# Strassen MLP on one core: four products held in PSUM banks over all chunks of a layer, banks given out by kind

## The chip, the cores and the metric

One Trainium2 chip; the program runs on one NeuronCore of it. The metric is device time in microseconds (us), the median of several executions. One further execution was recorded by the profiler; its own time stands beside its span below. Engines: TensorE (PE in the rows; PEld is its weight load), VectorE (DVE), ScalarE (ACT), GpSimd (POOL), SyncE (SP).

## The reference, cut to what matters

A decoder trunk of two layers on 256 tokens of width 2048, in float32. Each layer has a mixer (convolution and sparse attention in layer 0, causal pooling in layer 1) and then an MLP:

```python
def mlp(x, g, w1, w2):
    h = rmsnorm(x, g) @ w1          # 2048 -> 8192
    h = jnp.square(jax.nn.relu(h))
    return h @ w2                   # 8192 -> 2048
...
        x = x + mlp(x, mlp_norm[layer], w_mlp_in[layer], w_mlp_out[layer])
    return rmsnorm(x, final_norm)
```

## The kernel before

**Numbers in two parts.** Every weight tile W (128 x 2048, 1 MB) is streamed from HBM into `wraw` and split: ScalarE writes the rounded part `whi` (L147), VectorE the rest, `wlo = W - whi` (L152), in two halves of 1024 columns each. A product then needs three matmuls for each pair of blocks: x-high by W-high, x-high by W-low, x-low by W-high. There are three buffers each of `wraw`, `whi` and `wlo`.

**The MLP in chunks.** The hidden width of 8192 is cut into 8 chunks of 1024. For a chunk, the hidden tiles (`tile_of`: 48 matmuls of 256 columns into a bank, called *g* below) are computed one chunk ahead; `hidden` (L1023) takes the bank's relu and square into SBUF on ScalarE. The second matrix then multiplies the chunk's hidden values by seven products per half of the output (index `s`, two halves per chunk) instead of eight, in the way of Strassen and Winograd: two token blocks (of 128) by two output blocks of 512 columns. A *product* is 12 matmuls of 512 columns into one PSUM bank. Its inputs are the quarters of the hidden values (`f11`, `f12`, `f22`) or sums of them (`s1` to `s4`), each split in two by ScalarE (L1070) and VectorE (L1073); sums of weights are made in place on VectorE (`z += b`, `z += wraw`, L116) and by DMAs that add (L123, L127). The last of the eight chunks is done plainly, so the Strassen loop (L1143) makes seven passes per layer, c = 0 to 6, each of two halves, with 8 g and 14 products per pass. The flag `plain` marks the pass c = 6.

**What happens to a product.** PSUM has 8 banks of 128 x 512. `bank3` (L969) hands them out in turn. After each product, `update` (L1113) adds the bank, scaled for each token by 1/rms, onto the residual `x` in SBUF: one VectorE instruction of 128 x 512. A half makes seven updates. Three products accumulate in one bank A with f11 (`s2`, `s3`, `f22` after `f11`) and are added after each step, `s4` accumulates onto `s1` in bank C; the bank is added to one block after s1 and to another after s4. B holds f12.

**Order.** Each engine runs its instructions in the order in which the code issues them. `W.next()` (L170), called at the start of each g and product, first issues the loads of the unit four ahead and then the splits of all units up to two ahead; queued steps that make the inputs (`make`, `make_sum`) are put between the halves of the splits (L150). So in VectorE's order an update stands behind the splits that its product's `W.next()` issued, and ahead of those of the next unit. The order of one half, as TensorE sees it: f11, g, f12, s1, g, s2, s4, g, s3, g, f22.

Of the kernel before, what the change touches and what calls it, by code (L numbers as in the profile page):

```python
# [27 lines left out]
F32 = mybir.dt.float32  # L28
# [4 lines left out]
PSUM = bass.MemoryType.PSUM  # L33

P = 128
S = 256
# [143 lines left out]
def trunk(ctx: ExitStack, tc: tile.TileContext, a: dict, out: bass.AP, dump: dict | None = None):  # L180
# [10 lines left out]
    def mm(out, w, x, **kw):  # L191
        n = int(np.prod(x.shape[1:]))
        pe[0] += max(4 * n / 2400, 0.214) if x.dtype == F32 else max(n / 2400 + 0.0025, 0.107)
        nc.tensor.matmul(out, w, x, **kw)  # L194
# [81 lines left out]
    with ExitStack() as mx:  # L276
        mix = mx.enter_context(tc.tile_pool(name="mix", bufs=1, side="right", reuse_waits="tile"))
        ps1 = mx.enter_context(ExitStack())
        ps = ps1.enter_context(tc.tile_pool(name="ps1", bufs=1, space=PSUM, reuse_waits="tile"))

        def acc1(n=256, dt=F32):
            return ps.tile([P, 512], dt, tag="acc", bufs=8, name="acc")[:, 0:n]
# [181 lines left out]
        for pr in range(2):  # L464
            for i in range(2):
                acc = acc1()
# [140 lines left out]
        ps = ps2.enter_context(tc.tile_pool(name="ps2", bufs=1, space=PSUM, reuse_waits="tile"))  # L607
# [259 lines left out]
        for j in range(8):  # L867
# [5 lines left out]
            acc = ab[j][:, 0:256]  # L873
# [90 lines left out]
            nc.sync.dma_start(dump["o_tok"], o_tok)  # L964
        ps2.close()

        ps = ctx.enter_context(tc.tile_pool(name="ps3", bufs=1, space=PSUM, reuse_waits="tile"))

        def bank3():  # L969
            return ps.tile([P, 512], F32, tag="acc", bufs=8, name="acc")  # L970

        x = act.tile([P, 2, D], F32, tag="xr", bufs=1, name="x")
        turns = []
# [24 lines left out]
    def ssq_tile():  # L998
        return mlp.tile([P, 2, 4], F32, tag="ssq", bufs=2, name="ssq")

    def add_squares(dc, ssq):

        for tok in range(2):
            j = mlp.tile([P, 512], mybir.dt.bfloat16, tag="sq", bufs=1, name="sq")
            nc.scalar.activation(j, x[:, tok, dc * 512:(dc + 1) * 512], AF.Square, accum_out=ssq[:, tok, dc:dc + 1])
# [14 lines left out]
    def form(tag):  # L1020
        return mlp.tile([P, 1024], F32R, tag=tag, bufs=1, name=tag)

    def hidden(acc, out):  # L1023

        nc.scalar.activation(out, acc, AF.Relu)  # L1025
        nc.scalar.activation(out, out, AF.Square)  # L1026

    def unit_wide(acc):

        hi, lo = W.next(16)  # L1030
        for k in range(16):
            Xh, Xl = (xT[k // 4][:, k % 4, i * 256:(i + 1) * 256] for i in range(2))
            mm(acc, hi[:, k], Xh, start=(k == 0), stop=False)
            mm(acc, hi[:, k], Xl, start=False, stop=False)
            mm(acc, lo[:, k], Xh, start=False, stop=(k == 15))

    def t_tile():
        return mlp.tile([P, 4, 256], F32, tag="t", bufs=3, name="t")
# [24 lines left out]
    def quarter(c, tok, half):  # L1063
        return T[c, half][:, :, tok * P:(tok + 1) * P]

    def make(tag, src):

        def rounded():
            F[tag] = form(tag).rearrange("p (k t) -> p k t", k=4)
            nc.scalar.activation(F[tag][:, :, 0:P], src(), AF.Copy)  # L1070

        def rest():
            vector.tensor_sub(F[tag][:, :, P:2 * P], src(), F[tag][:, :, 0:P].bitcast(F32))  # L1073
            pending.remove(tag)

        pending.append(tag)
        W.queue += [rounded, rest]

    def make_sum(c, tag):
        def add():  # L1080
            s = sums[tag] = mlp.tile([P, 4, P], F32, tag="s", bufs=3, name="s")
            if tag == "s1":
                vector.tensor_sub(s, quarter(c, 1, 0), quarter(c, 1, 1))
            elif tag == "s2":
                vector.tensor_sub(s, sums["s1"], quarter(c, 0, 0))
            elif tag == "s3":
                vector.tensor_sub(s, quarter(c, 0, 0), quarter(c, 1, 0))
            else:
                vector.tensor_add(s, sums["s2"], quarter(c, 0, 1))

        W.queue.append(add)
        make(tag, lambda: sums[tag])

    def made(tag):
        while tag in pending:
            W.queue.pop(0)()
        return F[tag]

    def product(acc, tag, first):
        hi, lo = W.next()  # L1100
        X = made(tag)
        for k in range(4):
            xh, xl = X[:, k, 0:P], X[:, k, P:2 * P]
            mm(acc, xh, hi[:, k], start=(first and k == 0), stop=False, skip_group_check=True)
            mm(acc, xh, lo[:, k], start=False, stop=False, skip_group_check=True)
            mm(acc, xl, hi[:, k], start=False, stop=(k == 3), skip_group_check=True)

    def run_mlp(after, first):
        ssq = ssq_tile()
        r2 = const.tile([P, 2], F32, tag="r2", bufs=2, name="r2")  # L1110
        nr2 = const.tile([P, 2], F32, tag="nr2", bufs=2, name="nr2")

        def update(tok, dc, acc, r=r2):  # L1113
            o = x[:, tok, dc * 512:(dc + 1) * 512]
            vector.scalar_tensor_tensor(o, acc, r[:, tok:tok + 1], o, op0=ALU.mult, op1=ALU.add)

        def tile_of(c, j):

            if j % 4 == 0:
                T[c, j // 4] = t_tile()  # L1120
            acc = bank3()[:, 0:256]
            unit_wide(acc)
            hidden(acc, T[c, j // 4][:, j % 4])

        for _ in first():
            pass
        make("f11", lambda: quarter(0, 0, 0))
        make_sum(0, "s3")
        for j in range(4, 8):
            tile_of(0, j)  # L1130
            add_squares(j - 4, ssq)
        vector.reciprocal(r2, token_ms(ssq))
        vector.tensor_scalar(nr2, r2, -1.0, None, op0=ALU.mult)

        def second_half(c):
            make("f12", lambda: quarter(c, 0, 1))
            if c < CHUNKS - 1:
                for tag in ("s1", "s2", "s4"):
                    make_sum(c, tag)

        second_half(0)
        make("f22", lambda: quarter(0, 1, 1))
        for c in range(CHUNKS - 1):  # L1143
            plain = c + 1 == CHUNKS - 1
            for s in range(2):
                d0, d1 = 2 * s, 2 * s + 1
                A, C = bank3(), bank3()
                n = [4 * s]

                def g():  # L1150
                    tile_of(c + 1, n[0])
                    n[0] += 1

                product(A, "f11", True)
                update(0, d0, A)
                if s:
                    make("f11", lambda c=c: quarter(c + 1, 0, 0))
                g()
                B = bank3()
                product(B, "f12", True)  # L1160
                update(0, d0, B)
                product(C, "s1", True)
                update(1, d1, C)
                if s and plain:
                    make("s1", lambda c=c: quarter(c + 1, 1, 0))
                g()
                product(A, "s2", False)
                update(0, d1, A, nr2)
                product(C, "s4", False)
                update(0, d1, C)  # L1170
                g()
                product(A, "s3", False)
                update(1, d1, A, nr2)
                if s and not plain:
                    make_sum(c + 1, "s3")
                g()
                if s:
                    second_half(c + 1)
                product(A, "f22", False)
                update(1, d0, A)  # L1180
            make("f22", lambda c=c: quarter(c + 1, 1, 1))


        later = []
        for dc in range(4):
            acc = [bank3() for _ in range(2)]
            for half in range(2):
                hi, lo = W.next()
                X = [made(tag) for tag in (("f11", "s1"), ("f12", "f22"))[half]]
                order = [(k, tok) for k in range(4) for tok in range(2)]  # L1190
                if half:
                    order.sort(key=lambda o: o[1])
                for k, tok in order:
                    xh, xl = X[tok][:, k, 0:P], X[tok][:, k, P:2 * P]
                    mm(acc[tok], xh, hi[:, k], start=(half == 0 and k == 0), stop=False)
                    mm(acc[tok], xh, lo[:, k], start=False, stop=False)
                    mm(acc[tok], xl, hi[:, k], start=False, stop=(half == 1 and k == 3))
                if half == 0:
                    while later:
                        later.pop(0)()  # L1200
            for tok in range(2):
                update(tok, dc, acc[tok])
            later += after(dc)
        return later
# [104 lines left out]
    for h in range(2):  # L1309
        c = slice(h * 1024, (h + 1) * 1024)  # L1310
# [117 lines left out]
```

## Time and profile before

| | |
|---|---|
| median of 3 runs | 1772.74 us (1771.68 to 1776.7) |
| the profiled execution | 1777.96 us, span 1776.2 us |
| TensorE's granted clock over the span | 0.997 |
| busy shares | TensorE 99%, weight loads 90%, VectorE 85%, ScalarE 61%, GpSimd 3% |
| the MLP of layer 0, of layer 1 | about 392 to 1031 us and 1106 to 1731 us of the span |

The profiled execution lies 5.22 us above the median. Busy time of TensorE is modelled for pipelined matmuls, so 99% says that matmuls overlap without holes, not that they run at peak. The rows below are read as: start in us from the span's start, duration, engine, line, operation, output and inputs by the program's names; in brackets the engine's idle time before it and what ended that.

### The profile page before, as it was taken

What the parts mean: (1) busy time and instruction counts of PE and PEld (TensorE: products, weight loads), DVE (VectorE), ACT (ScalarE), POOL (GpSimd) and SP (SyncE); (2) the same over time, 40 slices, a digit from 0 to 9 for tenths busy, and PEclk for the clock granted to TensorE, in tenths of its full rate; (3) what the DMA queues carried; (4) which work ended last, traced back from release to release, by engine and by line L of the source; (5) the groups of instructions that cost most, each with busy time, mean ns of one, the idle gap of its engine ahead of it and who ended that gap; (6) DMA issues with size and microseconds to landing.
All of it is one profiled execution on the core that took longest, in us unless ns stands there. A gap on an engine that the chain in (4) does not pass through costs nothing.

```text
span 1776.2 us, 28729 instructions
## 1 busy us (share of the span) xinstructions
PE 1752.6 (99%) x11726; PEld 1595.4 (90%) x11726; DVE 1518.5 (85%) x1888; ACT 1084.6 (61%) x1626; POOL 59.7 (3%) x80
## 2 busy tenths in 40 slices
PE   9999999999999999999999999999999999999997
PEld 7999998889898899999898989988989898989885
DVE  6998997766989898898989868798988989898984
ACT  4445666547666666666666655766666666666663
POOL 1000000000000000000000000000000000000000
PEclk9999999999999999999999999999999999999998
DMA  7654323546778787878777764687878787778772
GB/s 274 237 197 143 120 96 134 199 167 227 259 248 253 236 248 236 276 230 295 232 248 247 230 228 155 232 256 238 257 237 271 233 294 233 249 243 259 247 245 97
DMA packets 58052, 399.89 MB, mean 225 GB/s; under 512 B 6560, under 2 KB 6960, under 8 KB 10816
## 3 DMA queue, kind: packets, MB, share of 16 engines
q1 hardware_dynamic: 47760, 333.47, 48.9%
q0 software_dynamic: 8576, 61.43, 18.5%
q10 hardware_dynamic: 1584, 3.16, 0.5%
q8 instruction: 92, 1.51, 0.3%
q14 instruction: 40, 0.33, 0.0%
HBM read 395.93 MB, written 2.10 MB: 224 GB/s over the span
## 4 chain that ended last, share of the span: by engine, by line
PE 78%; DVE 18%; ACT 2%; issue 1%; DMA 1%; ACTq 0%; POOLq 0%; SPq 0%; DVEq 0%
PE acc L194 73%; DVE wlo L78 9%; DVE z L78 3%; DVE s L78 3%; PE S L194 2%; DVE x L78 2%; PE PV L194 1%; ACT whi L147 1%; PE T L232 1%; PE acc L232 1%; DVE f L78 0%; DMA xraw<-in_xT 0%; ACT t L1026 0%; DMA ident<-in_ident 0%; ACT t L1025 0%
## 5 line engine op out<-in xcount | busy, mean ns | idle before, releaser
L194 PE MATMUL acc<-xT,whi 128*128 128x256 f32 x4992 | 872.1, 279 | 0.0
L194 PEld LDWEIGHTS acc<-xT,whi 128*128 128x128 f32 x4992 | 764.8, 188 | 10.1
L78 DVE TENSOR_TENSOR wlo<-wraw,whi 128x1024 fp32r<-128x1024 f32 (+1 forms) x552 | 604.9, 1126 | 143.7 <-ACT whi L147 142.8
L194 PE MATMUL acc<-xT,wlo 128*128 128x256 f32 x2496 | 694.0, 278 | 0.0
L147 ACT ACTIVATE whi<-wraw 128x1024 fp32r<-128x1024 f32 (+1 forms) x552 | 515.2, 974 | 105.1 <-PE acc L194 86.5
L194 PEld LDWEIGHTS acc<-xT,wlo 128*128 128x128 f32 x2496 | 470.7, 189 | 0.0
L194 PE MATMUL acc<-whi,s 128*128 128x512 f32 x960 | 318.5, 393 | 2.8 <-DVE s L78 1.6
L78 DVE TENSOR_TENSOR wlo<-z,whi 128x1024 fp32r<-128x1024 f32 x224 | 267.1, 1219 | 47.9 <-ACT whi L147 47.1
L147 ACT ACTIVATE whi<-z 128x1024 fp32r<-128x1024 f32 x224 | 230.5, 1054 | 94.2 <-DVE z L78 73.3
L194 PE MATMUL acc<-whi,f 128*128 128x512 f32 x864 | 283.0, 392 | 0.0
L194 PEld LDWEIGHTS acc<-whi,s 128*128 128x128 f32 x960 | 179.3, 188 | 42.2 <-DVE s L78 7.5
L1025 ACT ACTIVATE t<-acc 128x256 f32<-128x256 f32 x128 | 48.8, 381 | 251.6 <-PE acc L194 250.8
L194 PE MATMUL acc<-wlo,s 128*128 128x512 f32 x480 | 190.8, 397 | 1.1
L194 PEld LDWEIGHTS acc<-whi,f 128*128 128x128 f32 x864 | 162.4, 188 | 32.2
L194 PE MATMUL acc<-wlo,f 128*128 128x512 f32 x432 | 169.4, 392 | 0.0
L78 DVE SCALAR_TENSOR_TENSOR x<-acc,r,x 128x512 f32<-128x512 f32 x156 | 116.4, 746 | 14.4 <-PE acc L194 14.2
L194 PEld LDWEIGHTS acc<-wlo,s 128*128 128x128 f32 x480 | 90.1, 188 | 28.2 <-DVE wlo L78 9.7
L78 DVE SCALAR_TENSOR_TENSOR ctile<-ctile,cw 128x256 f32<-128x256 f32 x240 | 101.5, 475 | 0.1
L194 PEld LDWEIGHTS acc<-wlo,f 128*128 128x128 f32 x432 | 81.1, 188 | 16.0
L1070 ACT ACTIVATE s<-s 128x512 fp32r<-128x512 f32 x56 | 35.4, 632 | 72.1 <-DVE s L78 72.1
L78 DVE TENSOR_TENSOR z<-z,wraw 128x1024 f32<-128x1024 f32 x56 | 65.9, 1219 | 0.0
L78 DVE TENSOR_TENSOR z<-z,b 128x1024 f32<-128x1024 f32 x56 | 65.9, 1219 | 0.0
(206 smaller groups left out, 1361.4 us busy)
## 6 DMA issues: line engine op xcount, KB each, us to landing
wraw<-in_ws SPq DMA_DIRECT2D x254, 1024.0 KB, 6.3
z<-in_ws SPq DMA_DIRECT2D x28, 1024.0 KB, 7.4
b<-in_ws SPq DMA_DIRECT2D x28, 1024.0 KB, 4.8
b<-in_ws POOLq DMA_DIRECT2D x28, 1024.0 KB, 8.8
z<-in_ws POOLq DMA_DIRECT2D x28, 1024.0 KB, 8.2
xraw<-in_xT SPq DMA_DIRECT2D x4, 512.0 KB, 7.5
wraw<-in_ws SPq DMA_DIRECT2D x8, 256.0 KB, 7.4
w<-in_cmp_w POOLq DMA_DIRECT2D x2, 1024.0 KB, 7.6
```

The lines of the kernel that those rows point to most:

```text
L78: return fn(*args, **kw)
L147: nc.scalar.activation(hi[:, c], raw[:, c], AF.Copy)
L194: nc.tensor.matmul(out, w, x, **kw)
L232: nc.tensor.transpose(out, src, ident[0:n, 0:n])
L1025: nc.scalar.activation(out, acc, AF.Relu)
L1070: nc.scalar.activation(F[tag][:, :, 0:P], src(), AF.Copy)
```

## The change

Bank roles become fixed for the Strassen loop: the old pool is closed (`banks_for`), and a pool `strassen` gives two banks B (one per half), two banks S (`S1`, `S4`), two banks A, one C and one G, eight in all. The f12 products of both halves, and in half 0 the products s1 and s4, stay in banks of their own (B[0], B[1], S1, S4) over all seven passes: they start a bank only at c = 0 and are added to x only at c = 6. Since s4 no longer accumulates onto s1 there, S1 is added to two blocks at c = 6 and S4 to one. Half 1 keeps C as before. All g share the one bank G, where before each took the next of eight. After the loop a third pool (`ps4`) gives banks in turn again. Layer 1 goes through the same two pool changes. The products, the splits, the sums and the loads are unchanged in number and order.

```diff
--- before.py
+++ after.py
@@ -964,10 +964,18 @@
             nc.sync.dma_start(dump["o_tok"], o_tok)
         ps2.close()
 
-        ps = ctx.enter_context(tc.tile_pool(name="ps3", bufs=1, space=PSUM, reuse_waits="tile"))
-
-        def bank3():
-            return ps.tile([P, 512], F32, tag="acc", bufs=8, name="acc")
+        ps3 = ctx.enter_context(ExitStack())
+        banks = []
+
+        def banks_for(name):
+
+            ps3.close()
+            banks[:] = [ps3.enter_context(tc.tile_pool(name=name, bufs=1, space=PSUM, reuse_waits="tile"))]
+
+        def bank3(tag="acc", bufs=8):
+            return banks[0].tile([P, 512], F32, tag=tag, bufs=bufs, name="acc")
+
+        banks_for("ps3")
 
         x = act.tile([P, 2, D], F32, tag="xr", bufs=1, name="x")
         turns = []
@@ -1114,11 +1122,11 @@
             o = x[:, tok, dc * 512:(dc + 1) * 512]
             vector.scalar_tensor_tensor(o, acc, r[:, tok:tok + 1], o, op0=ALU.mult, op1=ALU.add)
 
-        def tile_of(c, j):
+        def tile_of(c, j, *bank):
 
             if j % 4 == 0:
                 T[c, j // 4] = t_tile()
-            acc = bank3()[:, 0:256]
+            acc = bank3(*bank)[:, 0:256]
             unit_wide(acc)
             hidden(acc, T[c, j // 4][:, j % 4])
 
@@ -1140,15 +1148,20 @@
 
         second_half(0)
         make("f22", lambda: quarter(0, 1, 1))
+
+        banks_for("strassen")
+        B = [bank3("B", 2) for _ in range(2)]
+        S1, S4 = (bank3("S", 2) for _ in range(2))
         for c in range(CHUNKS - 1):
             plain = c + 1 == CHUNKS - 1
             for s in range(2):
                 d0, d1 = 2 * s, 2 * s + 1
-                A, C = bank3(), bank3()
+                A = bank3("A", 2)
+                C = bank3("C", 1) if s else S1
                 n = [4 * s]
 
                 def g():
-                    tile_of(c + 1, n[0])
+                    tile_of(c + 1, n[0], "G", 1)
                     n[0] += 1
 
                 product(A, "f11", True)
@@ -1156,18 +1169,22 @@
                 if s:
                     make("f11", lambda c=c: quarter(c + 1, 0, 0))
                 g()
-                B = bank3()
-                product(B, "f12", True)
-                update(0, d0, B)
-                product(C, "s1", True)
-                update(1, d1, C)
+                product(B[s], "f12", c == 0)
+                if plain:
+                    update(0, d0, B[s])
+                product(C, "s1", s or c == 0)
+                if s or plain:
+                    update(1, d1, C)
                 if s and plain:
                     make("s1", lambda c=c: quarter(c + 1, 1, 0))
                 g()
                 product(A, "s2", False)
                 update(0, d1, A, nr2)
-                product(C, "s4", False)
-                update(0, d1, C)
+                product(C if s else S4, "s4", not s and c == 0)
+                if s or plain:
+                    update(0, d1, C)
+                if plain and not s:
+                    update(0, d1, S4)
                 g()
                 product(A, "s3", False)
                 update(1, d1, A, nr2)
@@ -1179,6 +1196,8 @@
                 product(A, "f22", False)
                 update(1, d0, A)
             make("f22", lambda c=c: quarter(c + 1, 1, 1))
+
+        banks_for("ps4")
 
 
         later = []
```

## Rows read from the trace of the kernel before

**Rows 1.** The page, parts 1 and 4: busy time and the chain by line.

```profile
PE 1752.6 (99%) x11726; PEld 1595.4 (90%) x11726; DVE 1518.5 (85%) x1888; ACT 1084.6 (61%) x1626; POOL 59.7 (3%) x80
...
PE acc L194 73%; DVE wlo L78 9%; DVE z L78 3%; DVE s L78 3%; PE S L194 2%; DVE x L78 2%; PE PV L194 1%; ACT whi L147 1%; PE T L232 1%; PE acc L232 1%; DVE f L78 0%; DMA xraw<-in_xT 0%; ACT t L1026 0%; DMA ident<-in_ident 0%; ACT t L1025 0%
```

**Rows 2.** The chain that ended last, in time: start, us, what.

```profile
534.05 58.60 PE acc L194 x394
...
787.45 57.36 PE acc L194 x394
...
1242.86 57.37 PE acc L194 x394
...
1326.09 57.37 PE acc L194 x394
```

**Rows 3.** Waits of TensorE's weight loads, 425 to 1730 us: total, times, longest.

```profile
PEld acc L194 <- DVE wlo L78: 9.7, 21, 0.6
PEld acc L194 <- DVE s L78: 7.5, 14, 1.2
```

**Rows 4.** Windows: stretch, length; busy PE, PEld, DVE, ACT, POOL; clock, DMA share, GB/s.

```profile
892.25:933.34 41.09, 41.09 (x278) 37.66 (x276) 36.21 (x38) 26.47 (x33) 1.70 (x2) 1.00 0.79 256
640.53:682.45 41.92, 41.92 (x277) 38.40 (x276) 36.30 (x38) 26.45 (x33) 1.71 (x2) 1.00 0.80 252
903.21:914.17 10.96, 10.96 (x74) 9.98 (x73) 10.53 (x12) 8.73 (x10) 0.85 (x1) 1.00 0.98 298
441.17:453.23 12.06, 11.25 (x73) 9.90 (x72) 12.06 (x14) 9.71 (x13) 0.85 (x1) 1.00 0.84 243
```

**Rows 5.** Timeline of the weight loads, pass c = 6 of layer 0.

```profile
951.49 0.19 PEld L194 LDWEIGHTS acc<-wlo,s 128*128 128x128 f32 x1 [0.39 <-DVE wlo L78]
...
953.28 0.19 PEld L194 LDWEIGHTS acc<-wlo,s 128*128 128x128 f32 x1 [0.57 <-DVE wlo L78]
953.89 0.30 PEld L194 LDWEIGHTS acc<-whi,s 128*128 128x128 f32 x2 [0.42 <-DVE s L78]
```

**Rows 6.** Timeline of VectorE before those waits.

```profile
929.86 2.36 DVE L78 TENSOR_TENSOR wlo<-wraw,whi 128x1024 fp32r<-128x1024 f32 x2 [1.72 <-ACT whi L147]
...
947.22 0.74 DVE L78 SCALAR_TENSOR_TENSOR x<-acc,r,x 128x512 f32<-128x512 f32 x1
947.88 0.68 DVE L78 TENSOR_TENSOR s<-s,s 128x512 fp32r<-128x512 f32 x1
...
951.36 0.74 DVE L78 SCALAR_TENSOR_TENSOR x<-acc,r,x 128x512 f32<-128x512 f32 x1
952.02 1.21 DVE L78 TENSOR_TENSOR wlo<-wraw,whi 128x1024 fp32r<-128x1024 f32 x1
```

**Rows 7.** Groups by line and form, VectorE: the updates.

```profile
L78 DVE SCALAR_TENSOR_TENSOR x<-acc,r,x 128x512 f32<-128x512 f32 x156 | 116.4, 746 | 14.4 <-PE acc L194 14.2
...
L78 DVE SCALAR_TENSOR_TENSOR x<-acc,nr,x 128x512 f32<-128x512 f32 x56 | 41.8, 746 | 0.0
```

**Rows 8.** Timeline of ScalarE, two relus of g and what follows.

```profile
951.82 0.36 ACT L1025 ACTIVATE t<-acc 128x256 f32<-128x256 f32 x1
...
961.99 0.39 ACT L1025 ACTIVATE t<-acc 128x256 f32<-128x256 f32 x1 [3.14 <-PE acc L194]
...
962.73 4.02 ACT L147 ACTIVATE whi<-z 128x1024 fp32r<-128x1024 f32 x4
```

**Rows 9.** Timeline of TensorE: an earlier change of pools, and a g.

```profile
335.39 0.40 PE L194 MATMUL S<-whi,yo 128*128 128x512 f32 x1
335.63 0.39 PE L194 MATMUL acc<-whi,yc 128*128 128x512 f32 x1
...
961.67 0.28 PE L194 MATMUL acc<-xT,wlo 128*128 128x256 f32 x1
...
964.53 0.28 PE L194 MATMUL acc<-xT,whi 128*128 128x256 f32 x1
```

## Prediction

> **What bounds the kernel now.** I read four views in this order. First the page: TensorE is busy 99% of the span, VectorE 85%, and the chain of work that ended last lies 73% on matmuls into banks and about 18% on VectorE's weight splits, sums and updates [rows 1]. So TensorE is nearly the bound, and VectorE sets the pace in places. The reader should ask how much TensorE really loses there, since a busy share cannot say it.
>
> Second, the chain in time. It repeats once per pass of the Strassen loop: some 57 us of matmuls, then a run of VectorE work, then matmuls again. From one entry to the next is the length of a pass: 1326.09 - 1242.86 = 83.23 us; in a stretch of layer 0 three passes take 787.45 - 534.05 = 253.40 us, 84.47 each [rows 2].
>
> Third, windows cut where TensorE does not wait. From the start of one g to the same g half a pass later it needs 41.09 us, so a pass without waiting is 2 x 41.09 = 82.18 us, and a pass of 83.23 us holds 1.05 us of waiting. In the stretch of layer 0 the half takes 41.92 us, a pass 83.84, and the waiting is 84.47 - 83.84 = 0.63 us [rows 4]. The whole loss is small: TensorE's weight loads waited 9.7 us for weight splits and 7.5 us for the inputs `s` over both MLPs [rows 3]; not all of that is lost, because a weight load normally runs ahead of its matmul. That is the most the change can touch. Shortening VectorE's work is worth only what TensorE waits for it.
>
> Fourth, one pass in detail. The three waits of a pass stand close together, at 951.49, 953.28 and 953.89 us, in the products s2 and s4 of half 0, and all end on VectorE [rows 5]. VectorE's last idle time before them is the 1.72 us ahead of 929.86, where it waits for ScalarE; from there to the waits it is dense [rows 6], because both weight sums, four input sums and the normal splits fall together. It slowly loses its lead of two units, and TensorE catches up with it. Later in the pass it gains the lead back.
>
> **The change, part by part.** *Updates removed.* A half has seven updates. In passes 0 to 5 half 0 loses three (f12, s1, s4) and half 1 one (f12); pass 6 has one more than before, since S1 and S4 go into one block separately. Per layer 6 x 4 - 1 = 23, together 46 of the 212 updates (156 with r, 56 with -r) [rows 7]: 46 x 0.746 = 34.3 us of VectorE time. The -r updates stay 56, those with r should become 110.
>
> *What that buys.* Only what stands ahead of the waits. In VectorE's order the update of f12 (947.22) and that of s1 (951.36) lie between its last idle time and the waits, and each takes up 0.66 us of the queue (947.88 - 947.22, 952.02 - 951.36) [rows 6]. The first wait has one removed update ahead of it: 0.66 us against a wait of 0.39. The second and third have two: 1.32 us against 1.05 us of delay in all. Both margins are 0.27 us, so I take the waits of such a pass as gone, whole. VectorE's start into the dense stretch is set by ScalarE, which fills a `whi` buffer when TensorE has freed it, so it moves with TensorE and does not use up the margin.
>
> The shown pass is c = 6 of layer 0, and it is the one in which these updates remain. Its neighbours are alike in length, so the sum goes by pass: c = 6 keeps its 1.05 us in both layers; its added update stands behind the waits, where VectorE regains its lead, and costs nothing; if that cover were gone it would be 0.66 us, twice. Pass c = 0 loses more in one place: g, s1, s2, then the next start of g take 12.06 us where 10.96 is the length without waiting, so 1.10 us [rows 4], with the same two updates ahead of it (1.32 us).
>
> *The sum.* Where all passes have the short length: 2 x 1.10 + 10 x 1.05 = 12.7 us. In the profiled execution three waiting passes of layer 0 have the longer length, so 2 x 1.10 + 7 x 1.05 + 3 x 0.63 = 11.4 us, and it would become 1777.96 - 11.4 = 1766.5 us. Its three longer passes cost 3 x (84.47 - 83.23) = 3.7 us of the 5.2 by which it lies above the median, so I take the median execution to have none of them. The median then goes from 1772.74 to 1760.0 us. The rest of the 34.3 us becomes idle time of VectorE.
>
> *Accumulating over passes.* A product that adds onto an old bank is what s2, s3 and f22 do already on A; their matmuls are among those of the 41.09 us. Nothing, from both sides.
>
> *Pool changes.* Four new ones (two per layer). The nearest row is the first matmul into the pool before: it starts 0.24 us after its forerunner, in the normal stream, with no wait [rows 9]. The banks taken first were last used several units earlier. The upper bound is one relu at the border, 0.2 us of latency and 0.39 us of work [rows 8], four times: 2.4 us. I take the row, 0.
>
> *One bank for all g.* Now a g waits for the relu of the g before. The closest pair has one product between them: the last matmul of a g starts at 961.67, its relu runs 961.99 to 962.38, the next g starts at 964.53 [rows 8, 9]; 2.15 us to spare. Where ScalarE is late (951.82), two products lie between. Nothing, unless the bank comes back later than its relu ends (below).
>
> Here the Trainium skill speaks against the change. Its page "Perfetto Trace Analysis" says under "Optimizing Tensor Performance" that independent groups of matmuls should rotate through different banks, so that the emptying of one overlaps the matmuls of the next, and under "Optimization Strategy" that the same gap repeating on the engine that should be saturated can mean too little PSUM. By that rule the gap of each pass would grow. The rows of the waits disagree: what ends them is a split or a sum on VectorE, never a bank.
>
> **The rivals.**
> *A longer pitch of TensorE.* The two pass lengths differ though nothing waits more: same instructions, granted clock 1.00 in both (the 2.4 GHz level), but a half takes 41.92 us against 41.09 [rows 4]. In the trace the longer pitch begins and ends at the waits, and holds in between. If passes without waits keep the pitch they start with, a layer can be caught in either. One layer's six passes: 6 x (83.84 - 82.18) = 10 us back, 1770 us, no difference worth the name. This is the case that can end on the slow side: all passes long add 12 x 1.66 + 2 x 1.24 = 22.4 us, 1782 us; it outweighs the gain from about eight of 14 passes on. For it: three of 14 passes show it, without a cause that the profile names. Against: both layers enter their loop in the short pitch, after unchanged work.
>
> *Another wait takes the place.* The inputs s2 and s4 go VectorE, ScalarE, VectorE; if ScalarE's part is what is late, taking updates away shifts nothing. Against: VectorE has no idle time in the dense stretch. If half the waiting stays, 1766 us; if all, 1773.
>
> *Bank G comes back late.* If G were free only after the work that ScalarE does behind the relu (962.73 + 4.02 = 966.75 [rows 8]) instead of at 962.38, each closest pair would lose 966.75 - 964.53 = 2.2 us, 28 times: 62 us, some 1822 us. It decides once the release comes over 2.15 us late. By the skill's rule on rotation this is where it would show. Against: the relu is an instruction of its own that can give the bank back.
>
> **How the numbers follow.** A measurement of this kernel can tell about 0.3%, 5.3 us, from no change; so faster means below 1767.4. Waits gone and at most four long passes (1756 to 1767): 0.68. Half the waits stay (1766): 0.08, counted 0.06 faster and 0.02 same. One layer long (1770): 0.12. No gain (1773): 0.04. Most passes long (1782): 0.05. Bank G late (1822): 0.03. Together faster 0.74, same 0.18, slower 0.08. Range: from 1756, if the median before held three long passes that go (3.7 us), up to 1771, past the one long layer; it leaves out the last three cases, 0.12. Predicted: 1760 us.
>
> **What would show it.** Right: passes c = 1 to 5 last 82.2 us (83.8 in the long pitch) with no wait of the weight loads, c = 6 still shows 1.05 us and its three waits, updates are 110 and 56, VectorE's busy time falls by 34 us, and 961.99's relu still precedes the next g by 2 us. Wrong: the waits are still there but end on ScalarE; TensorE waits at the start of a g for a relu; or pass lengths near 83.8 without waits, which is the pitch.

## The result, and the profile after

The changed kernel takes 1761.23 us (median of 6 runs, 1758.13 to 1762.95); before takes 1775.51 us in the same comparison (6 runs, 1771.68 to 1778.08). The ratio is 0.9925, interval 0.9914 to 0.9937. In medians that is 14.3 us less, in the ratio 13.3; forecast were 12.7 us and 1760.0. The profiled execution has a span of 1758.7 us, against 1776.2.

The page of the changed kernel, parts 1 and 4, answers to [rows 1]:

```profile
PE 1740.3 (99%) x11726; PEld 1592.6 (91%) x11726; DVE 1489.1 (85%) x1842; ACT 1084.6 (62%) x1626; POOL 59.8 (3%) x80
...
PE acc L194 90%; PE S L194 2%; DVE wlo L78 2%; PE PV L194 1%; PE T L232 1%; PE acc L232 1%; DVE z L78 1%; DVE s L78 0%; DVE x L78 0%; PE T L194 0%; DMA vec<-in_vec 0%; DVE ctile L78 0%; ACT whi L147 0%; DVE csum L78 0%; DVE yo L78 0%
```

VectorE has 46 instructions less. The share of the chain that lies on TensorE's matmuls into banks goes from 73% to 90%, and the splits, sums and updates almost leave it. The busy shares, 99 and 85%, tell nothing of that.

Its chain in order of time (start, us, what), the pieces of over 40 us that touch the MLPs, against [rows 2]:

```profile
388.62 525.81 PE acc L194 x3612
...
940.29 77.84 PE acc L194 x478
...
1094.14 520.34 PE acc L194 x3564
...
1640.35 105.31 PE acc L194 x598
```

Where the chain left TensorE once in every pass, it now stays on it over six passes, 3564 matmuls without a break in layer 1. It leaves it once per layer, in pass 6. The waits of the weight loads in both MLPs, against [rows 3], and the place of those of layer 0, against [rows 5]:

```profile
PEld acc L194 <- DVE wlo L78: 1.9, 4, 0.6
PEld acc L194 <- DVE s L78: 0.8, 2, 0.4
```

```profile
937.89 0.19 PEld L194 LDWEIGHTS acc<-wlo,s 128*128 128x128 f32 x1 [0.39 <-DVE wlo L78]
...
939.69 0.19 PEld L194 LDWEIGHTS acc<-wlo,s 128*128 128x128 f32 x1 [0.58 <-DVE wlo L78]
940.29 0.30 PEld L194 LDWEIGHTS acc<-whi,s 128*128 128x128 f32 x2 [0.42 <-DVE s L78]
```

Of 35 waits six are left, three in each pass 6, of the same sizes as in [rows 5]. Windows of the changed kernel (stretch, length, busy PE, PEld, DVE, ACT, POOL, clock, DMA): a whole pass of layer 1, then half a pass of layer 0 ahead of pass 6's waits and one behind them:

```profile
1239.00:1321.19 82.19, 82.19 (x554) 75.30 (x553) 72.80 (x74) 53.33 (x68) 3.45 (x4) 1.00 0.80 256
867.69:908.78 41.09, 41.09 (x277) 37.65 (x276) 34.43 (x34) 25.40 (x32) 1.71 (x2) 1.00 0.85 280
951.14:993.06 41.92, 41.92 (x277) 38.39 (x276) 36.18 (x36) 25.93 (x33) 1.71 (x2) 1.00 0.83 274
```

A pass takes 82.19 us; 82.18 was worked out from [rows 4]. The two lengths of a half of [rows 4] are here too, the longer one only behind the waits. The groups of updates, against [rows 7], and VectorE in pass 5 of layer 0, where the two updates of [rows 6] stood:

```profile
L78 DVE SCALAR_TENSOR_TENSOR x<-acc,r,x 128x512 f32<-128x512 f32 x110 | 82.0, 746 | 14.5 <-PE acc L194 14.2
...
L78 DVE SCALAR_TENSOR_TENSOR x<-acc,nr,x 128x512 f32<-128x512 f32 x56 | 41.7, 745 | 0.0
```

```profile
849.16 2.35 DVE L78 TENSOR_TENSOR z<-z,wraw 128x1024 f32<-128x1024 f32 x2
851.43 0.69 DVE L78 TENSOR_TENSOR s<-s,s 128x512 fp32r<-128x512 f32 x1
...
853.78 1.22 DVE L78 TENSOR_TENSOR wlo<-z,whi 128x1024 fp32r<-128x1024 f32 x1
854.91 1.22 DVE L78 TENSOR_TENSOR wlo<-wraw,whi 128x1024 fp32r<-128x1024 f32 x1
```

Between the weight sum and the next input, and between the two splits, there is no update any more; the splits follow each other at once.

### The profile page after: what moved, and what is told of

It reads as the page before. It is cut to its first block, busy times and chain, and to the rows that moved or that the text cites. A ratio compares the mean times of both kernels' runs of the same rounds, so it can differ in the third digit from the quotient of the medians.

```text
span 1758.7 us, 28659 instructions
## 1 busy us (share of the span) xinstructions
PE 1740.3 (99%) x11726; PEld 1592.6 (91%) x11726; DVE 1489.1 (85%) x1842; ACT 1084.6 (62%) x1626; POOL 59.8 (3%) x80
## 4 chain that ended last, share of the span: by engine, by line
PE 95%; DVE 3%; ACT 1%; DMA 0%; issue 0%; ACTq 0%; POOLq 0%; DVEq 0%
PE acc L194 90%; PE S L194 2%; DVE wlo L78 2%; PE PV L194 1%; PE T L232 1%; PE acc L232 1%; DVE z L78 1%; DVE s L78 0%; DVE x L78 0%; PE T L194 0%; DMA vec<-in_vec 0%; DVE ctile L78 0%; ACT whi L147 0%; DVE csum L78 0%; DVE yo L78 0%
## 5 line engine op out<-in xcount | busy, mean ns | idle before, releaser
L78 DVE SCALAR_TENSOR_TENSOR x<-acc,r,x 128x512 f32<-128x512 f32 x110 | 82.0, 746 | 14.5 <-PE acc L194 14.2
```

Of the source, the lines that this page charges most:

```text
L78: return fn(*args, **kw)
```

## The experiments

Theory: the gain is VectorE's time ahead of the waits, and nothing else. Rivals: VectorE's load counts wherever it is taken; or the gain comes from the banks themselves (fewer handovers and starts on TensorE). Each experiment was built from the changed kernel and compared with before on its own chip: the first three runs on one chip (before 1776.65 us), the other three on another (before 1778.2 us).

**The same number of updates taken out, ahead of the waits or behind them.** The first holds the f12 of half 0 alone, the second that of half 1 alone. The edit of the first (the second has `s != 1`):

```diff
-        S1, S4 = (bank3("S", 2) for _ in range(2))
...
-                C = bank3("C", 1) if s else S1
+                C = bank3("C", 2)
...
-                product(B[s], "f12", c == 0)
-                if plain:
+                product(B[s], "f12", c == 0 or s != 0)
+                if plain or s != 0:
                     update(0, d0, B[s])
-                product(C, "s1", s or c == 0)
-                if s or plain:
-                    update(1, d1, C)
+                product(C, "s1", True)
+                update(1, d1, C)
...
-                product(C if s else S4, "s4", not s and c == 0)
-                if s or plain:
-                    update(0, d1, C)
-                if plain and not s:
-                    update(0, d1, S4)
+                product(C, "s4", False)
+                update(0, d1, C)
```

> Only the f12 product of half 0 is held over the passes; s1 and s4 share a bank again, f12 of half 1 is added in each pass. 12 updates fewer than before, each ahead of the waits of its pass. Theory (what counts is the queue of VectorE ahead of the waits): in passes 0 to 5 of both layers 0.66 us is taken off; the first wait goes, 1.05 - 0.66 = 0.39 us stays at the later ones. 12 x 0.66 = 7.9 us less than before, ratio about 0.9955. Rival (VectorE's load counts wherever it is taken): a quarter of the 46 updates, a quarter of the 13.3 us, 3.5 us less, ratio 0.998.

> Only the f12 product of half 1 is held. Again 12 updates fewer, each behind the waits of its pass, where VectorE has its lead back. Theory: the waits of a pass stay as before, 1.05 us, and the time too: ratio 1.000, not over 1 us either way. Rival (load counts wherever it is taken): 3.5 us less, ratio 0.998, as in the run with half 0.

Ahead of the waits: 1769.41 us, ratio 0.9963 (0.9949 to 0.9977), 7.2 us less in medians where 7.9 were expected. Behind them: 1774.73 us, ratio 0.999 (0.9977 to 1.0003), 1.9 us less in medians where at most 1 was expected; this interval alone does not exclude the rival's 0.998, but the pass lengths do. The chain in time, from one entry to the next; first for half 0, then for half 1:

```profile
1151.27 57.36 PE acc L194 x394
...
1233.83 57.36 PE acc L194 x394
```

```profile
1410.36 57.37 PE acc L194 x394
...
1493.59 57.37 PE acc L194 x394
```

In the short pitch (the 41.09 us half of [rows 4]) the pass takes 82.56 us with half 0 held, 0.38 over the pass without waits (0.39 was expected), and 83.23 with half 1 held, as in [rows 2]. The weight loads of the first at the end of that pass show which wait went:

```profile
1233.23 0.19 PEld L194 LDWEIGHTS acc<-wlo,s 128*128 128x128 f32 x1 [0.15 <-DVE wlo L78]
1233.83 0.30 PEld L194 LDWEIGHTS acc<-whi,s 128*128 128x128 f32 x2 [0.42 <-DVE s L78]
```

The first of the three waits is gone, the second is 0.15 us instead of 0.57, the third is as it was. One instruction of 0.66 us in the queue is worth 0.66 us per pass ahead of the waits and, by the pass lengths, nothing behind them.

**The same banks, but VectorE's time given back.**

```diff
+        def instead():
+            vector.scalar_tensor_tensor(spare, spare, r2[:, 0:1], spare, op0=ALU.mult, op1=ALU.add)
...
                 if plain:
                     update(0, d0, B[s])
+                else:
+                    instead()
                 product(C, "s1", s or c == 0)
                 if s or plain:
                     update(1, d1, C)
+                else:
+                    instead()
```

and the same once more after s4. `spare` is a buffer of 128 x 512 in SBUF. The 48 instructions put in are the updates of passes 0 to 5 that the change takes out; the two that it adds in the passes 6 stay.

> The banks are held as in the change, but in each place where an update was taken out VectorE does a throwaway instruction of the same kind and size on a spare buffer in SBUF. Theory (VectorE's time is all the gain): the waits of passes 0 to 5 come back, about 1 us each, and the time is that of before, ratio 1.000 (0.998 to 1.002). Rival (the gain comes from the banks themselves, fewer handovers and starts on TensorE): the time stays that of the change, ratio 0.9925.

1777.3 us, ratio 1.0008 (0.9994 to 1.0023): the whole gain is gone, though all four products are still held. The group of throwaway instructions in its profile, then two entries of its chain:

```profile
L78 DVE SCALAR_TENSOR_TENSOR spare<-spare,r 128x512 f32<-128x512 f32 x48 | 36.0, 750 | 0.0
```

```profile
1323.07 57.36 PE acc L194 x394
...
1406.31 57.37 PE acc L194 x394
```

In the short pitch passes are back at 83.24 us. Holding the banks has no gain of its own on TensorE; that rival falls.

**The change once more, and with the additions of pass 6 moved.** In pass 6 the sums of B[0] and S1 still stand ahead of the waits. The second kernel moves two of them, with the work unchanged:

```diff
                 product(B[s], "f12", c == 0)
-                if plain:
+                if plain and s:
                     update(0, d0, B[s])
                 product(C, "s1", s or c == 0)
-                if s or plain:
+                if s:
                     update(1, d1, C)
...
                 update(1, d1, A, nr2)
+                if plain and not s:
+                    update(0, d0, B[0])
+                    update(1, d1, S1)
```

> The change as it is, for the chip of the next two runs. Ratio 0.9925 (0.9914 to 0.9937). Pass lengths of 82.2 us in passes 1 to 5 and a rest of 1.05 us of waits in pass 6 of each layer.

> The change, and in pass 6 the additions of B[0] and of S1 to the second token block are moved from ahead of the waits to behind the product s3 of half 0, where the profile of the change shows VectorE idle for 2.65 us. Theory: the waits of pass 6 go in both layers, 2 x 1.05 = 2.1 us; and if the pitch of TensorE is drawn anew only at waits, it also stays short to the end of the loop, where the change shows the long one after pass 6's waits in both layers (6 of 8 g and 10 of 14 products, about 1.25 us per layer): 4.6 us less than the change in all, ratio to before 0.990. Rival (the work is only moved, and its cover is too short): VectorE is late for the next half instead, waits of the same 1.3 us there, ratio as the change, 0.9925.

The change: 1759.21 us, ratio 0.9889 (0.9874 to 0.9904), below the 0.9914 to 0.9937 that was expected; the next part takes that up under *The size*. With the sums moved: 1755.82 us (1755.43 to 1756.13), ratio 0.987 (0.9854 to 0.9887), 3.4 us less than the change on the same chip. The chain of the kernel with the moved sums, all its pieces of over 40 us in the MLPs:

```profile
388.81 627.16 PE acc L194 x4248
...
1091.99 649.21 PE acc L194 x4320
```

Each layer's Strassen loop is one unbroken run of matmuls; the list of waits of the weight loads between 420 and 1725 us is empty. It is the fastest kernel of the study. Of the forecast 4.6 us, 2.1 are waits, and these are shown: from the first f11 of a loop to its end, the two loops together take 1152.7 us in this chip's profile of the change and 1150.6 here. The rest of the forecast hung on the pitch, which in that profile of the change stayed short after pass 6. That the timed runs of the change ran there in the long pitch more often, which would put the 3.4 us between the two sums, is not shown.

**One bank A instead of two.**

```diff
-                A = bank3("A", 2)
+                A = bank3("A", 1)
...
-                    tile_of(c + 1, n[0], "G", 1)
+                    tile_of(c + 1, n[0], "G", 2)
```

> The change with one bank A for both halves and two banks G. Theory (a single bank is free of cost only where the engine that empties it is not behind): at each half's end f11 of the next half must wait until VectorE has added f22 from A; in the profile of before that update ran some 3.8 us after f22's last matmul had begun its end, because splits and a weight sum stand ahead of it. So 2 to 4.5 us at 26 borders of halves, 50 to 115 us more than the change. Rival (the order of the queue gives the update early enough, as it does the relu of G): under 5 us more.

1931.84 us, ratio 1.086 (1.0837 to 1.0883): 173 us more than the change, above the expected range of 50 to 115. TensorE's waits for updates, then its timeline at one border of halves, VectorE's there, and windows of TensorE behind that wait:

```profile
PE acc L194 <- DVE x L78: 118.0, 26, 4.5
```

```profile
705.42 0.40 PE L194 MATMUL acc<-whi,f 128*128 128x512 f32 x1
710.35 0.77 PE L194 MATMUL acc<-whi,f 128*128 128x512 f32 x1 [4.54 <-DVE x L78]
```

```profile
709.46 0.74 DVE L78 SCALAR_TENSOR_TENSOR x<-acc,r,x 128x512 f32<-128x512 f32 x1
```

```profile
710.35:717.30 6.95, 6.95 (x31) 5.95 (x32) 4.91 (x6) 1.93 (x3) 0.59 (x1) 0.69 1.01 218
717.30:722.00 4.70, 4.70 (x37) 4.46 (x37) 2.74 (x4) 1.74 (x4) 0.00 (x0) 1.00 0.53 223
```

The last matmul of f22 starts at 705.42 us; the update that empties A waits in VectorE's queue behind splits and a weight sum until 709.46 and ends at 710.20; f11 of the next half starts only behind it, at 710.35. That is the 4.54 us, and 26 such waits make 118. What the expectation left out stands in the last windows: behind the wait, in which TensorE had stood still, the granted clock is 0.69 on average over 6.95 us, a mix of its two levels (1.2 and 2.4 GHz), then 1.00 again, all at the upper one. At 0.69 those 6.95 us cost 6.95 x 0.31 = 2.2 us more. Together 6.7 us per border; 26 borders make 174. The Trainium skill says the same of the clock in "TensorE: Matmul & The Clock Gate", Part 1: an idle TensorE falls to 1.2 GHz and activity releases it; this run agrees.

## Why the prediction was right

*The loss was waiting on VectorE, about 1.05 us per pass.* Right: in both layers all passes 1 to 5 take 82.19 us, as worked out, where before they took 83.23 in the short pitch.

*What counts is the work ahead of the waits; both margins are 0.27 us.* Right, and measured apart: 0.66 us ahead of the waits gave 7.2 us in the run, behind them nothing that can be told from zero. With half of the cut ahead, the remainder was 0.38 us against 0.39 worked out. One reading was off: VectorE's dense stretch before the waits holds three input sums, not four; no term rests on it.

*34.3 us of VectorE time, 12.7 of them worth something.* The count is right, 110 and 56 updates, and VectorE's instructions are 46 less. Its busy time fell by 29.4 us (1518.5 to 1489.1) and not 34.3: rows of neighbours overlap, and 0.66 us, the place in the queue, is the size to use here too (46 x 0.66 = 30.4).

*Pass 6 keeps its waits.* Right, all three in both layers; moving its sums took them away.

*Pool changes cost nothing, at most one relu of 0.59 us each.* In the change no wait on ScalarE is recorded in the MLPs. In the two runs that hold one product, where the pool had seven banks, the first f11 of layer 1 did wait for a relu. TensorE's waits in the one that holds half 0:

```profile
PE acc L194 <- ACT t L1033: 0.5, 1, 0.5
```

So such a wait does occur and is about as long as the upper bound; why the eight banks of the change avoid it was not tested.

*One bank for all g is enough.* Right. The closest pair in the changed kernel, ScalarE's relu and TensorE's next g, against [rows 8, 9]:

```profile
865.14 0.39 ACT L1033 ACTIVATE t<-acc 128x256 f32<-128x256 f32 x1 [2.73 <-PE acc L194]
```

```profile
867.69 0.28 PE L194 MATMUL acc<-xT,whi 128*128 128x256 f32 x1
```

The bank is free at 865.53, 2.16 us early. The run with one bank A shows the other side: there the engine that empties the bank has a queue, and one bank costs 6.7 us each time. The rule of the Trainium skill ("Perfetto Trace Analysis", "Optimizing Tensor Performance") that groups should rotate through banks holds for A and not for G, by when the emptying instruction's turn comes.

*The pitch.* The rival was rightly described for the loops: passes without waits hold the pitch they start with. In these profiles it took nothing from the gain but added to it (*The size*). In the profiles of all kernels but the one with a single A, read from the starts of the g, every change of pitch inside a Strassen loop stands right behind a wait: 17 changes at 60 groups of waits, none elsewhere. An example is the chain of the run that holds f12 of half 1, a long pass that begins and ends at a wait:

```profile
1242.64 58.60 PE acc L194 x394
...
1327.11 57.38 PE acc L194 x394
```

1327.11 - 1242.64 = 84.47 us, where its neighbours take 83.23. The changed kernel has no wait in twelve of its 14 passes and is in the short pitch through all of them; behind pass 6's waits it is long in both layers in its first profile and short in its second.

*The size.* Measured were 14.3 us in the first comparison and 19 on the second chip (1778.2 to 1759.21), whose ratio interval lies below the first one's; 12.7 were forecast for an execution before without a long pass. The profiles show what is waiting and what is pitch. The loop of layer 1 is in the short pitch throughout, in before and in the second profile of the change. From its first f11 to its end, first before, then the change:

```profile
1136.28:1718.96 582.68, 580.53 (x3866) 525.82 (x3865) 525.33 (x541) 374.78 (x476) 24.17 (x28) 1.00 0.79 251
```

```profile
1122.53:1698.88 576.35, 576.12 (x3866) 526.86 (x3865) 510.76 (x518) 374.86 (x476) 24.16 (x28) 1.00 0.80 254
```

That is 6.33 us; for two layers 12.7, the forecast. The spans of the first two profiles differ by 17.5 us. Of these 13.8 lie in the two loops: the 11.4 us of waits that the prediction worked out for this execution, and 2.4 of pitch (three long passes before, two stretches behind the waits of pass 6 after). The other 3.6 us lie ahead of the loops, where the change touches nothing: the first f11 starts at 427.47 us before and at 423.83 after. Most of it is pitch again: fifteen groups of 48 matmuls of 256 columns, which the mixer of layer 0 runs in a row, before and after:

```profile
42.69:127.49 84.80, 84.80 (x722) 84.80 (x721) 83.32 (x151) 37.85 (x52) 1.98 (x5) 1.00 0.61 223
```

```profile
42.39:123.99 81.60, 81.60 (x723) 81.60 (x721) 81.60 (x147) 38.09 (x52) 2.21 (x6) 1.00 0.62 223
```

The run that holds f12 of half 1, with the mixer of the changed kernel, has the longer time here too (84.80 us); so it is not the change that shortens it. Here one step of the prediction does not hold. It put 3.7 of the 5.2 us by which the profiled execution lay above the median down to the three long passes, and took the median to have none. With the mixer's 3.6 us beside them, an execution before without stretches in the long pitch would take about 1777.96 - 3.7 - 3.6 = 1770.7 us (an estimate), 2 us less than the base of 1772.74; the lowest of the measured ones is 1771.68. With the waits gone that would be 1758.0. The changed kernel in turn has long stretches behind the waits of its passes 6, 2.5 us in its first profile. So the saving by the waits is right, and that 1760.0 met 1761.23 so closely is in part luck with the pitch. How many long stretches the timed executions had stays open: they have no trace.

## What to carry to other kernels

When TensorE loses its time at one place of a loop, read the queue of the late engine between its last idle time and that place: an instruction there is worth its place in the queue, up to the length of the wait, the same instruction elsewhere nothing. PSUM can be spent on this, by letting sums stay in banks over a loop, and before giving a role a single bank one checks when the emptying instruction's turn comes in its engine's order, not how long it takes. Work that must be done once can be moved to where its engine idles; that gave the fastest kernel here.

## What the runs showed of the hardware that was not expected

TensorE's matmuls of 256 columns run at two pitches with the granted clock at 1.00 in both (the 2.4 GHz level): a half of a pass takes 41.09 or 41.92 us, fifteen groups of 48 of them in the mixer 81.60 or 84.80. Inside the Strassen loops the pitch changed only behind a wait. Kernels with waits in each pass spread more than the one without: on the second chip before took 1776.9 to 1781.97 us in 7 runs, the kernel with the moved sums 1755.43 to 1756.13. These are 4 runs only. What sets the pitch is open.
